# The first load of a streaming sum of reciprocals, made in two transfers

## The chip, the cores and the metric

The kernel runs on one core of a Trainium2 chip. Its time is the device time of one execution in microseconds; where several runs are compared, the median counts. The core has a tensor engine (PE), a vector engine (DVE), a scalar engine (ACT), a general engine (POOL) and an engine that here only issues transfers (SP). Sixteen DMA engines move data between the chip's main memory and the core's own memory.

## The reference

The input has 32 x 512 rows of 1024 positive float32 numbers, 67.1 MB. The output is one number per row:

```python
def reference(x: np.ndarray) -> np.ndarray:
    return np.sum(1.0 / x, axis=-1).astype(np.float32)
```

## The kernel before, in words

The 16384 rows are dealt to 128 partitions, 128 rows to each, so "row r" below means 128 rows of the input, one per partition. A partition's rows lie one after the other in main memory, so that a load of n rows is one run of n x 4096 bytes in each partition.

**The arithmetic.** A row is cut into halves a and b of 512 columns, and 1/a + 1/b is worked out as (a + b) / (ab), so that one reciprocal serves two elements. The product ab is made by POOL (token P, line 197), or for a few rows by DVE (tokens V and W, line 218). ACT makes the reciprocal of the product as exp(-ln(ab)): token L (line 240) is the logarithm and E (line 249) the exponential. DVE then multiplies, sums along the row and writes one number (token R, line 265, followed by a short read of the accumulator). Rows go one of two ways at the end. In the first, E writes the reciprocal to a bank of the matmul memory (E with @bank), and R multiplies it with both halves of the row. In the second, PE adds the halves a + b in a bank by two matmuls with an identity matrix (token S, line 230), E writes in place, and R multiplies the two. Where DVE makes the product, PE mostly copies the second half into a bank first (token C, line 207), so that DVE reads one operand from there.

**The order.** All of it is written out in one string, PLAN (lines 37 to 72). Each token is one step; its letter names the operation, the number the row, +2 two rows at once and @n the bank. Each engine carries out its own tokens strictly in the order in which they stand. An engine that waits at a token therefore holds up all its later ones. Which instruction waits for which is worked out by `note` (lines 133 to 162), row by row: a reader of a row waits for the one transfer that brings it.

**The loads.** Token Dn (lines 179 to 191) loads the next n rows into a ring of 40 rows. SP issues them on one queue, in order. The first three tokens load 12, 15 and 13 rows and fill the ring without a wait; each later load waits on SP until the rows that it overwrites have been used. The transfers take eight completion semaphores in turn, so that a transfer also waits for the one issued eight before it. Loads grow smaller towards the end, down to half rows: the last two rows are treated as four units of half the width.

**Around the change.** The first tokens after the loads are P0+2, C3@3, S2@0, V3, P2, L0, L1, C11@3, S3@1, E0@6, E1@7, P4+2, V11, L2, L3, R0, S6@2, E2, E3, R1. So POOL's first three steps are P0+2, P2 and P4+2; PE's are C3, S2, C11, S3 and S6; DVE's are V3, V11, R0 and R1. Rows 0 to 3 are used by P0+2, C3, V3, P2, S2 and S3, and later by R0 to R3; row 11 is used by C11 and V11.

Of the kernel before, what the change touches and what calls it, by code (L numbers as in the profile page):

```python
# [11 lines left out]
def kernel(  # L12
# [22 lines left out]


    PLAN = """
        D12 D15 D13 P0+2 C3@3 S2@0 V3 P2 L0@0 L1@1 C11@3 S3@1 E0@6 E1@7 P4+2 V11 L2@3 L3@2
        R0 S6@2 E2 E3 R1 P6+2 L4+2@4 R2 R3 E4+2@6 S7@0 P8+2 L6+2@8 R4 S10@1 E6+2 R5 D7 P10
        L8+2@10 R6 R7 S11@2 E8+2@6 L10+2@6 R8 E10+2 R9 R10 R11 P12+2 C19@3 S14@0 V19 P14+2  # L40
        L12+2@12 S15@1 E12+2@6 S18@2 R12 P16+2 L14+2@16 R13 E14+2 R14 P18 L16+2@18 R15 S19@0
# [271 lines left out]
```

## Time and profile before

| | us |
|---|---|
| time, median of 9 runs | 169.22 (168.93 to 169.68) |
| the profiled execution's own time | 169.26 |
| its span | 167.2 |
| PE, ACT, POOL, DVE busy in the span | 132.6, 132.9, 128.1, 128.0 |
| load of the first 12 rows, from issue to landing | 17.4 |
| load of the next 15 rows, from issue to landing | 35.1 |
| load of the next 13 rows, from issue to landing | 50.4 |

The span is the time from the first to the last thing that the profile records on the core; the execution's own time is 2.06 us longer. "Busy" counts the time in which an engine carries out instructions; an engine that waits at a semaphore is idle. A chain of waits names, from the last instruction back, what released each step; where a transfer is named, the time from its issue to its landing is shown, whether it moved or stood in the queue. A landing is the moment at which the transfer's semaphore is complete, that is, when the last of the 16 DMA engines has finished its share. Each DMA engine carries the same eight partitions of a transfer, one packet for each partition.

### The profile page before, as it was taken

The numbers are of one execution on the slowest core, as the hardware profiler recorded it, in microseconds if no ns is written. First come the engines' busy times: TensorE is split into PE (matmuls) and PEld (weight loads), VectorE is DVE, ScalarE is ACT, GpSimd is POOL, SyncE is SP. The second block draws the span as 40 slices with busy tenths as digits, with TensorE's granted clock in tenths as the row PEclk, the third lists the DMA queues.
The fourth block names the chain that finished last, engine by engine and source line by source line (L and its number), as shares of the span: only waits on it lengthen the run. The fifth ranks groups of instructions, "written<-read, shape, count | busy, mean of one in ns | idle before, by whom it ended". The sixth has DMA issues, their size and how long they took to land.

```text
span 167.2 us, 1332 instructions
## 1 busy us (share of the span) xinstructions
PE 132.6 (79%) x292; PEld 54.8 (33%) x292; DVE 128.0 (77%) x283; ACT 132.9 (79%) x161; POOL 128.1 (77%) x80
## 2 busy tenths in 40 slices
PE   0000699939989999977998999999799669989692
PEld 0000243314433434322433434344244133424261
DVE  0000129863789989887798898799999989999994
ACT  3000096926999999986999997999899999999992
POOL 1000699129999999949999997966899997979970
PEclk9999999996999999999999999999999999999999
DMA  6998999999998999999999999999999999999910
GB/s 200 470 459 376 470 470 470 411 403 446 433 408 365 432 445 415 470 396 439 423 447 431 431 404 437 431 437 423 411 439 420 408 425 412 427 406 411 396 73 16
DMA packets 4616, 67.26 MB, mean 402 GB/s; under 512 B 512, under 2 KB 640, under 8 KB 2176
## 3 DMA queue, kind: packets, MB, share of 16 engines
q1 hardware_dynamic: 4608, 67.18, 94.8%
q14 instruction: 6, 0.05, 0.1%
q8 instruction: 2, 0.03, 0.1%
HBM read 67.11 MB, written 0.07 MB: 402 GB/s over the span
## 4 chain that ended last, share of the span: by engine, by line
DMA 50%; DVE 17%; POOL 11%; issue 8%; PE 8%; ACT 4%; DVEq 0%; SPq 0%; ACTq 0%; POOLq 0%
DMA ring<-in_x_dram 50%; POOL prod L197 11%; DVE ring L265 10%; PE ps L230 5%; DVE prod L265 4%; PE ps L207 3%; DVE prod L218 2%; ACT prod L240 2%; ACT ps L249 1%; DVE sums L265 1%; ACT prod L249 1%; DVEq L308 0%; SPq L185 0%; ACTq L240 0%; POOLq L197 0%
## 5 line engine op out<-in xcount | busy, mean ns | idle before, releaser
L197 POOL TENSOR_TENSOR prod<-ring 128x1024 f32<-128x1024 f32 (+2 forms) x74 | 127.4, 1753 | 33.8 <-DMA ring<-in_x_dram 31.8
L230 PE MATMUL ps<-ring,ident 128*128 128x512 f32 (+1 forms) x260 | 117.7, 600 | 5.4 <-DVE sums L265 4.2
L240 ACT ACTIVATE prod<-prod 128x1024 f32<-128x1024 f32 (+2 forms) x80 | 69.1, 876 | 27.4 <-POOL prod L197 26.5
L265 DVE CUSTOM_DVE_ANT_1 ring<-ring,ps 128x1024 f32<-128x1024 f32 (+1 forms) x65 | 76.4, 1209 | 8.8 <-ACT ps L249 8.8
L230 PEld LDWEIGHTS ps<-ring,ident 128*128 128x128 f32 x260 | 49.1, 194 | 72.8 <-issue 50.9
L265 DVE CUSTOM_DVE_ANT_0 prod<-prod,ps 128x512 f32<-128x512 f32 (+1 forms) x63 | 40.6, 678 | 1.2 <-ACT prod L249 1.2
L207 PE MATMUL ps<-ring,ident 128*128 128x512 f32 x32 | 18.4, 666 | 26.1 <-DMA ring<-in_x_dram 26.1
L249 ACT ACTIVATE ps<-prod 128x1024 f32<-128x1024 f32 (+2 forms) x40 | 33.9, 854 | 2.4 <-DVE sums L265 1.6
L249 ACT ACTIVATE prod<-prod 128x1024 f32<-128x1024 f32 (+2 forms) x40 | 34.6, 875 | 0.8
L218 DVE TENSOR_TENSOR prod<-ring,ps 128x512 f32<-128x512 f32 x16 | 10.9, 686 | 26.8 <-PE ps L207 26.6
L207 PEld LDWEIGHTS ps<-ring,ident 128*128 128x128 f32 x32 | 5.7, 201 | 36.1 <-issue 21.5
L265 DVE DVE_READ_ACCUMULATOR2_ANT sums<- 128x1 f32 x130 | 10.8, 83 | 0.0
L218 DVE TENSOR_TENSOR prod<-ring 128x512 f32<-128x512 f32 (+1 forms) x7 | 4.3, 635 | 0.0
L83 ACT ACT_TABLE_LOAD x1 | 1.3, 1283 | 0.7 <-PEq L297 0.7
L265 DVE CUSTOM_DVE_ANT_0 prod<-prod,ps,sums 128x256 f32<-128x256 f32 x2 | 0.9, 478 | 0.0
masks.py:197 POOL MEMSET ident<- 128x128 f32 x1 | 0.2, 205 | 0.3 <-POOLq L297 0.3
masks.py:199 POOL TENSOR_SCALAR_AFFINE_SELECT ident<-ident 128x128 f32<-128x128 f32 x1 | 0.3, 294 | 0.1
L297 POOL MEMSET const-float32-0.0<- 128x1 f32 x1 | 0.1, 100 | 0.2 <-issue 0.2
L297 POOL MEMSET const-bfloat16-1.0<- 128x1 bf16 x1 | 0.1, 103 | 0.0
L297 POOL MEMSET const-uint8-127<- 128x1 uint8 x1 | 0.1, 103 | 0.0
L297 POOL MEMSET const-float32-1.0<- 128x1 f32 x1 | 0.1, 100 | 0.0
## 6 DMA issues: line engine op xcount, KB each, us to landing
ring<-in_x_dram SPq DMA_DIRECT2D x2, 4096.0 KB, 32.3
ring<-in_x_dram SPq DMA_DIRECT2D x1, 7680.0 KB, 35.1
ring<-in_x_dram SPq DMA_DIRECT2D x2, 3584.0 KB, 30.1
ring<-in_x_dram SPq DMA_DIRECT2D x1, 6656.0 KB, 50.4
ring<-in_x_dram SPq DMA_DIRECT2D x1, 6144.0 KB, 17.4
ring<-in_x_dram SPq DMA_DIRECT2D x3, 2048.0 KB, 34.6
ring<-in_x_dram SPq DMA_DIRECT2D x2, 3072.0 KB, 32.3
ring<-in_x_dram SPq DMA_DIRECT2D x1, 5120.0 KB, 27.2
```

What stands on the lines that cost most here:

```text
L83: nc.scalar.add_instruction(mybir.InstLoadActFuncSet(name=nc.get_next_instruction_name(), act_func_set_id=act_sets.index("natural_log_exp_ ...
L197: inst = nc.gpsimd.tensor_tensor(out=prod[:, p : p + m, :w], in0=ring[:, a : a + m, at : at + w], in1=ring[:, a : a + m, at + w : at + 2 * w],
L207: inst = nc.tensor.matmul(ps[:, b, : place(r)[2]], lhsT=ident, rhs=xs(r, 1), start=True, stop=True,)
L218: inst = nc.vector.tensor_tensor(out=prod[:, p, :w], in0=xs(r, 0), in1=in1, op=mult)
L230: inst = nc.tensor.matmul(ps[:, b, : place(r)[2]], lhsT=ident, rhs=xs(r, h), start=h == 0, stop=h == 1,)
L240: inst = nc.scalar.activation(out=pg, in_=pg, func=Ln, scale=S)
L249: inst = nc.scalar.activation(out=rc, in_=pg, func=Exp, scale=-1.0)
L265: inst = nc.vector.tensor_tensor_reduce(out=row, in0=row, in1=other, scale=S, scalar=total if q in summed else 0.0, op0=mult, op1=add, acc ...
L297: nc = _bacc.Bacc("TRN2", target_bir_lowering=False, num_devices=1)
```

## The change

The first load of 12 rows is issued as two loads, of 4 and of 8 rows. Every other token and its place stay the same, and the order on PE, DVE, ACT and POOL is unchanged. SP issues 32 loads instead of 31. What waits for what follows: the users of rows 0 to 3 wait for the first transfer, those of rows 4 to 11 for the second. Each later transfer takes the next semaphore in turn, and its wait is for the transfer eight before it in the new count.

```diff
     PLAN = """
-        D12 D15 D13 P0+2 C3@3 S2@0 V3 P2 L0@0 L1@1 C11@3 S3@1 E0@6 E1@7 P4+2 V11 L2@3 L3@2
+        D4 D8 D15 D13 P0+2 C3@3 S2@0 V3 P2 L0@0 L1@1 C11@3 S3@1 E0@6 E1@7 P4+2 V11 L2@3 L3@2
         R0 S6@2 E2 E3 R1 P6+2 L4+2@4 R2 R3 E4+2@6 S7@0 P8+2 L6+2@8 R4 S10@1 E6+2 R5 D7 P10
```

## The prediction

> **What bounds the kernel now.** I read, in this order: the slices and DMA queue of the page, to see whether any resource is full all the time; the timeline of POOL, PE, ACT and DVE around the first landings, to see what an earlier landing could move; the chain that ended last; and the queue of SP, to see whether a load is ever issued too late.
>
> The page's span, its DMA slices and its queue row come first.
>
> ```profile
> span 167.2 us, 1332 instructions
> ...
> DMA  6998999999998999999999999999999999999910
> ...
> q1 hardware_dynamic: 4608, 67.18, 94.8%
> ```
>
> The load queue is busy 94.8% of 167.2 us, 158.5 us, and its only slack is before the first packet and in the last slices. All 16 DMA engines stream from about 1.75 us to the last landing at 161.49 us. No compute engine passes 79%.
>
> Next the timeline at the first two landings, one engine after the other: POOL, PE, ACT, DVE.
>
> ```profile
> 18.25 11.79 POOL L197 TENSOR_TENSOR prod<-ring 128x1024 f32<-128x1024 f32 x6 [16.94 <-DMA ring<-in_x_dram]
> 36.38 24.69 POOL L197 TENSOR_TENSOR prod<-ring 128x1024 f32<-128x1024 f32 x12 [6.35 <-DMA ring<-in_x_dram]
> ...
> 28.05 5.52 PE L230 MATMUL ps<-ring,ident 128*128 128x512 f32 x12 [0.24 <-DVE sums L265]
> 36.36 1.68 PE L207 MATMUL ps<-ring,ident 128*128 128x512 f32 x2 [2.79 <-DMA ring<-in_x_dram]
> ...
> 33.59 1.06 ACT L249 ACTIVATE prod<-prod 128x1024 f32<-128x1024 f32 x1
> ...
> 36.12 0.08 DVE L265 DVE_READ_ACCUMULATOR2_ANT sums<- 128x1 f32 x1
> ```
>
> Columns: start, duration, engine, line, count, and idle time before with its releaser. The 12 rows land at 18.2 us. POOL has multiplied them by 30.03, PE has finished at 33.57, ACT at 34.65, and DVE reads its last accumulator at 36.12 to 36.20. The 15-row load lands at 36.31. So at 36.3 every engine has finished every row it has, and waits for data.
>
> Then the last long DMA piece of the chain, and SP's issues between 28 and 60 us.
>
> ```profile
> 100.06 34.96 DMA ring<-in_x_dram
> 135.02 0.14 issue
> 135.16 1.10 PE ps L207 x2
> ...
> 31.02 21.39 SPq L185 DMA_DIRECT2D ring<-in_x_dram  x3
> ```
>
> The end hangs on the landing at 135.02 us: PE copies and sums from it, DVE takes over and runs almost without a gap to 164.8. The issue at 100.06 is not what made that landing late, since 35 us of transfers stood ahead of it in the queue. The three issues of rows 40 to 63 come at 31.02, 46.81 and 52.08, while the first 40 rows land until 52.06 and the next 7 and 10 rows until 60.8 and 74.0: so the queue still holds 21, 14 and 22 us of transfers at those moments. The last load of all is issued at 153.80 and lands at 161.49. An earlier issue cannot make the stream earlier.
>
> **The change, part by part.** The profiled execution took 169.26 us, span 167.2 and 2.06 around it; the median of the nine runs is 169.22, so sums against 169.26 stand 0.04 high.
>
> 1. *One more issue on SP.* The first three take 0.38 to 0.42 us each, at 0.74, 1.18 and 1.65. The issues of the 15 and 13 rows move back by about 0.45 us, to 1.65 and 2.1. They are needed at 18 and 36 us, so the cover is 16 us and the cost is 0. The first issue stays at 0.74.
>
> 2. *More packets in the stream.* From the trace's record of each DMA packet: the 12 rows of one partition are one packet of 49,152 bytes, 128 such packets in all, eight on each DMA engine. After the change each DMA engine has eight of 16,384 and eight of 32,768 instead. Shortest packets of those sizes elsewhere in the trace: 0.611, 1.213 and 1.815 us. So 0.611 + 1.213 - 1.815 = 0.009 us per partition, with the usual 0.613 for the small one 0.011, times eight = 0.09 us per engine. One more completion packet adds 0.009 us. Between transfers nothing else is paid: the 15 rows land 18.14 us after the 12, and 8 x 2.267 us are 18.14. Cost 0.1 us on the full stream, with nothing beside it: the landing at 36.31 and all later ones move to +0.1.
>
> 3. *The start of the stream.* The first packet of each engine took 2.18 to 2.90 us, 0.6 us more than 1.815 in the mean; the second and later ones 1.815 to 1.92. I price it as paid once, as before: 0. Bounds: it shrinks with the packet to a third (-0.4), or is paid again by the first packets of the second transfer (+0.6). I take 0 because the first packets of the 15-row load, which also follow a transfer on a running queue, take 2.267 like all their others.
>
> 4. *Rows 0 to 3 land early.* First packets begin at 1.75 to 2.78; 0.6 + 8 x 0.613 = 5.5 us later, plus 0.3 us from last packet to semaphore (17.83 to 18.17 before), gives about 8.6 us. What can then run: POOL's product of rows 0 and 1 (2.35 us) and row 2 (1.28), PE's copy of row 3 and sum of row 2 (18.31 to 23.5, 5.2 us), DVE's V3, ACT's logs and exponentials of rows 0 to 3.
>
> 5. *Two waits move to the second transfer.* POOL's P4 waits for the 8 rows: behind it all POOL products, and ACT's L4. PE's C11 waits for them: behind it S3, though its row is there, and then S6 and S7. DVE's V11 waits for C11, and R0 to R3 stand behind V11. So no reduction of a row runs before 18.3 either. All that is won by then is 3.6 us of POOL, 5.2 us of PE and 4.5 us of ACT. POOL ends its first 12 rows at about 18.3 + 8.3 = 26.6 instead of 30.0, DVE its last of them some 3 to 5 us before 36.2.
>
> 6. *What is late next.* At 36.4 all engines wait for the 15 rows, exactly as before; POOL's wait grows from 6.35 to about 9.8 us and nothing else changes. The ring slots come free earlier, so the 7-row load is issued at about 27 instead of 31.02, behind 25 us of queue instead of 21. Value 0.
>
> 7. *PE's clock.* The granted clock is 0.50 from 36.80 to 40.20 us, after PE's pause of 2.79. A longer pause can put the drop ahead of 36.4, so that the first copy takes 2.04 us (as at 18.31) instead of 1.68. V19 on DVE then starts 0.4 late, but DVE's next operation waits 2.15 us for ACT, which covers it. Cost 0; without that cover 0.4.
>
> Sum: 0 + 0.1 + 0 + 0 + 0 = +0.1 us, 169.26 + 0.1 = 169.36, less the 0.04 to the median: **169.3 us**.
>
> The Trainium skill (Perfetto Trace Analysis, DMA Optimizations) says that splitting transfers may let the task end sooner if the DMA engines are generally idle; here the row reads 94.8% busy, so the rule's condition fails, and with it the gain. The same skill (DMA: Bandwidth & Descriptors, Anatomy of one DMA) gives about 2.0 us of fixed cost for each DMA; if the stream paid that, the sum would be 171.3 us, but landings 18.14 us apart for 18.14 us of packets show that a queued transfer pays none of it here.
>
> **The rivals.**
>
> - *The second transfer pays a start of its own* (slower). Place: the first packets of the 8 rows, at about 7 us. Price 0.6, with step 2 +0.7: 169.9 us. It decides over the forecast from 0.25 us of excess on the slowest engine. For: no trace shows a small packet at the very start of the stream, where the packets took 0.6 us too long. Against: the 15- and 13-row loads start without it.
> - *The head start survives* (faster). If the engines did not run dry at 36.3, POOL's 3.6 us would travel on to the end: 169.3 - 3.6 = 165.7. Against: 6.35 us of idle POOL and 2.79 us of idle PE before 36.4, waiting for DMA, and again 2.49 us of POOL at 74.1.
> - *A luckier order of the DMA engines* (slightly faster). Engines end the first transfer between 16.93 and 17.83 us, and a landing waits for the last. If smaller first packets even this out by half, -0.45: 168.9. For: step 3's excess differs by 0.7 us between engines. Against: the start order, which the issue sets, remains.
> - *The clock of PE* (slower): step 7 without its cover, +0.1 + 0.4: 169.7.
> - *The change does nothing at all*: 169.2, not to be told from the forecast.
>
> **How the numbers follow.** Forecast with the idle case 64%; second start 14%; clock 6%; luckier engines 11%; head start 5%. A measurement of this kernel tells about 0.2% (0.34 us) from no change. Forecast: 61 same, 3 slower. Second start: 12 slower, 2 same. Clock: 5 slower, 1 same. Engines: 8 faster, 3 same. Head start: 5 faster. Together faster 0.13, same 0.67, slower 0.20. The likeliest case alone is 169.0 to 169.6. The range takes in the luckier engines and the second start and leaves out the head start: 168.8 to 169.9.
>
> **What would show it.** Right: a first landing at 8 to 9 us, a second at 18.2 to 18.4, the 15 rows at 36.3 to 36.6; POOL idle some 10 us before that; the last landing 0.1 us later. Wrong: a first packet of the second transfer above 1.3 us; the 15 rows landing before 36.0 or after 36.8; an engine still at work on the first 12 rows when they land; or an end that moves apart from the landing at 135.02.

## The result

| | before | after |
|---|---|---|
| time, median | 169.41 us (31 runs, 168.93 to 170.16) | 168.86 us (10 runs, 168.78 to 169.02) |
| ratio, 95% interval | | 0.9968 (0.9958 to 0.9978) |
| the profiled execution: time, span | 169.26, 167.2 | 168.86, 167.1 |
| last load landed | 161.49 us | 161.25 us |
| output issued | 164.86 us | 164.64 us |

The change makes the kernel 0.55 us faster, 0.32%. The first nine of the 31 runs are those of the table before the change (169.22), on which the forecast was built; against them the gain is 0.36 us. The forecast was 169.3 us and no measurable change. The time lies inside the stated range and next to one of the rivals (168.9), but the sign of the most likely case was missed.

The page of the kernel after, its span, DMA slices, packets and load queue:

```profile
span 167.1 us, 1335 instructions
...
DMA  5999999999999998999999999999999999999910
...
DMA packets 4760, 67.26 MB, mean 403 GB/s; under 512 B 528, under 2 KB 656, under 8 KB 2192
...
q1 hardware_dynamic: 4752, 67.18, 94.7%
```

The queue carries 144 packets more than before (4752 against 4608): those that step 2 counted, 128 of data and 16 of completion. It is as full as it was (94.7% against 94.8%).

The timeline of POOL, PE and DVE after, up to the first product of the 15-row load (start, duration, and in brackets the idle time before, with what ended it):

```profile
8.18 3.57 POOL L197 TENSOR_TENSOR prod<-ring 128x1024 f32<-128x1024 f32 x2 [6.88 <-DMA ring<-in_x_dram]
17.86 8.23 POOL L197 TENSOR_TENSOR prod<-ring 128x1024 f32<-128x1024 f32 x4 [6.10 <-DMA ring<-in_x_dram]
36.00 2.34 POOL L197 TENSOR_TENSOR prod<-ring 128x1024 f32<-128x1024 f32 x1 [9.91 <-DMA ring<-in_x_dram]
...
35.98 2.08 PE L207 MATMUL ps<-ring,ident 128*128 128x512 f32 x2 [6.64 <-DMA ring<-in_x_dram]
...
31.71 0.08 DVE L265 DVE_READ_ACCUMULATOR2_ANT sums<- 128x1 f32 x1
```

The head start is there, and it is absorbed: POOL's wait for the 15 rows grew from 6.35 to 9.91 us, DVE stops at 31.79 instead of 36.20. But the two landings themselves are earlier. POOL starts on the 15 rows at 36.00 instead of 36.38, and on rows 4 to 11 at 17.86, while it had rows 0 to 11 at 18.25 before.

The DMA view of the first 3 us after, with the loads issued in them (size, time from issue to landing):

```profile
ring<-in_x_dram SPq DMA_DIRECT2D x1, 7680.0 KB, 34.3
ring<-in_x_dram SPq DMA_DIRECT2D x1, 6656.0 KB, 49.6
ring<-in_x_dram SPq DMA_DIRECT2D x1, 4096.0 KB, 16.6
ring<-in_x_dram SPq DMA_DIRECT2D x1, 2048.0 KB, 7.4
```

With issues at 0.74, 1.16, 1.63 and 2.10 us these are landings at 8.11, 17.79, 35.94 and 51.69. Before, 12, 15 and 13 rows landed at 18.17, 36.31 and 52.06. The stream runs 0.37 us ahead although it carries 0.1 us more packets, and it does so from the first 12 rows on.

The chain that ended last, and the issue of the output, after:

```profile
99.73 35.08 DMA ring<-in_x_dram
134.81 0.14 issue
134.95 1.10 PE ps L207 x2
...
164.64 0.34 SPq L282 DMA_DIRECT2D out_dram<-sums  x1
```

The landing that stood at 135.02 us is now at 134.81, 0.21 us earlier, and the issue of the output moves with it, from 164.86 to 164.64. So the end still hangs on the stream, as the prediction read it.

### The profile page after: what moved, and what is told of

Its sections match the earlier page's. It is cut to its first block, busy times and chain, and to the rows that moved or that the text cites. A ratio compares the mean times of both kernels' runs of the same rounds, so it can differ in the third digit from the quotient of the medians.

```text
span 167.1 us, 1335 instructions
## 1 busy us (share of the span) xinstructions
PE 134.1 (80%) x292; PEld 55.9 (33%) x292; DVE 128.3 (77%) x283; ACT 133.0 (80%) x161; POOL 128.1 (77%) x80
## 3 DMA queue, kind: packets, MB, share of 16 engines
q1 hardware_dynamic: 4752, 67.18, 94.7%
## 4 chain that ended last, share of the span: by engine, by line
DMA 60%; DVE 16%; PE 15%; issue 3%; ACT 2%; SPq 1%; DVEq 0%; ACTq 0%
DMA ring<-in_x_dram 60%; PE ps L230 11%; DVE ring L265 10%; DVE prod L265 4%; PE ps L207 4%; DVE prod L218 2%; ACT prod L240 1%; DVE sums L265 1%; ACT prod L249 1%; ACT ps L249 1%; SPq L185 1%; DVEq L308 0%; ACTq L240 0%
## 5 line engine op out<-in xcount | busy, mean ns | idle before, releaser
L230 PEld LDWEIGHTS ps<-ring,ident 128*128 128x128 f32 x260 | 50.0, 196 | 72.4 <-issue 52.9
L207 PE MATMUL ps<-ring,ident 128*128 128x512 f32 x32 | 19.8, 709 | 25.4 <-DMA ring<-in_x_dram 25.4
L207 PEld LDWEIGHTS ps<-ring,ident 128*128 128x128 f32 x32 | 5.9, 212 | 35.2 <-issue 16.8
```

Source lines behind the costliest of these rows:

```text
L207: inst = nc.tensor.matmul(ps[:, b, : place(r)[2]], lhsT=ident, rhs=xs(r, 1), start=True, stop=True,)
L230: inst = nc.tensor.matmul(ps[:, b, : place(r)[2]], lhsT=ident, rhs=xs(r, h), start=h == 0, stop=h == 1,)
```

## The experiments

Two theories stood at the outset. **A, the start:** the slowest of the 16 DMA engines gets through its first packets sooner when they are short, and the end follows the stream. **B, the head start:** work done on early rows reaches the end in some way that the waits do not show. After the first four runs a third was needed. **C, outside the span:** part of the gain is time that the profile's span does not contain. "Outside the span" below is an execution's time less its own span, as a mean over a kernel's runs; it was 1.86 us in the ten runs of the changed kernel. "Too long" is the time of a packet over the usual time of its size in the same trace. The packet records do not name the DMA engine; the first 16 packets by start are taken as the first of each of the 16 engines. The spread is the time between the first and the last of the 16 engines that report a landing.

**The kernel before, once more.**

> The kernel before, unchanged, for a second profile of it and for the width of the comparison. Theory A (the slowest DMA engine starts the stream more slowly when the first packets are long; the end follows): ratio 1.000 within 0.001; first packets of 49,152 bytes again 0.5 to 0.8 us too long in the mean; the 12 rows land between 18.1 and 18.5 us. Theory B (the early rows let the engines run ahead) says the same of this run. If the 12 rows land at 17.8 here, A has lost its evidence, since the profile before would then have been a late one by chance.

Median 169.27 us, ratio 0.9996 (0.9987 to 1.0006). The 12 rows landed at 18.14 us, first packets were 0.63 us too long in the mean (0.64 in the first profile), and the 16 DMA engines reached that landing with a spread of 0.94 us (0.87). The late landing of before is no accident of one profile.

**The first 12 rows as 1 and 11.**

```diff
-        D12 D15 D13 P0+2 ...
+        D1 D11 D15 D13 P0+2 ...
```

> The first 12 rows in transfers of 1 and 11 rows. No step of any engine can use row 0 alone (POOL's first product is of rows 0 and 1, PE's first copy of row 3), so there is no head start at all, but the first packets are short, 4,096 bytes. Theory A: first packets at most 0.4 us too long in the mean, the 12 rows land at 17.6 to 17.9 us, time 0.3 to 0.6 us below the kernel before, ratio 0.9965 to 0.998. Theory B: no head start, no gain: ratio 1.000 to 1.001 (the additional packets cost 0.1 us).

168.97 us, ratio 0.998 (0.9971 to 0.9989). First packets of 4,096 bytes were 0.28 us too long in the mean, and the 12 rows landed at 17.65 us. The first packets of the 11-row transfer behind them, from 3.31 us on, were 0.13 us too long in the mean and up to 0.42, so here the start was not paid by the very first packets alone. The mean span fell by 0.17 us. There is a gain in the span with no early row that any step can use. That is A; B expected none.

**The first 12 rows as 8 and 4.**

```diff
-        D12 D15 D13 P0+2 ...
+        D8 D4 D15 D13 P0+2 ...
```

> The first 12 rows in transfers of 8 and 4 rows. First packets of 32,768 bytes, between those of the two kernels; eight rows land at about 12.5 us, so that three of POOL's products and all that hangs on rows 0 to 7 except what stands behind C11 on PE can run early. Theory A: first packets 0.45 to 0.6 us too long in the mean, the 12 rows land at 17.9 to 18.2 us, ratio 0.998 to 1.000. Theory B: POOL's head start is larger than with 4 rows (5 us against 3.6), so the gain is at least that of the change: ratio 0.997 or less.

169.17 us, ratio 0.9992 (0.9982 to 1.0001). First packets of 32,768 bytes were 0.57 us too long, the spread was 0.90 us, and the 12 rows landed at 18.25 us, slightly later than A expected. POOL's timeline in this run:

```profile
13.43 11.78 POOL L197 TENSOR_TENSOR prod<-ring 128x1024 f32<-128x1024 f32 x6 [12.13 <-DMA ring<-in_x_dram]
36.47 4.66 POOL L197 TENSOR_TENSOR prod<-ring 128x1024 f32<-128x1024 f32 x2 [11.26 <-DMA ring<-in_x_dram]
```

POOL is 4.8 us ahead of the kernel before, and its wait grows to 11.26 us. The mean span, 167.29 us, equals that of the kernel before in the same comparison (167.30). The larger head start is worth nothing: B falls.

**A small load ahead of the 12 rows.**

```diff
     with tc.manual_schedule():
+        nc.sync.dma_start(out=sums, in_=x_v[:, F - 1, :F])
         for op, r, n, b in ops:
```

> An additional load of 128 columns (512 bytes per partition, into the sums, which are overwritten later) is issued ahead of the load of 12 rows; all else as before. It costs 8 x 0.027 us of stream, and the 12 rows are issued about 0.45 us later. No head start. Theory A in the form that only the very first packets of the stream pay: the 49,152-byte packets take 1.82 to 1.95 us from the first on, and the 12 rows land at 17.9 to 18.2 us: ratio 0.998 to 1.000. Theory A in the form that long packets are slow at the start whatever stands before them: they take 2.4 us again, the 12 rows land at 18.6 to 18.8, ratio 1.002 to 1.004. Theory B: no head start, later landing, ratio 1.001 to 1.003.

169.67 us, ratio 1.0022 (1.0013 to 1.0031). The first 512-byte packets paid next to nothing (0.029 us against 0.025), and the 49,152-byte packets behind them, starting at 2.25 to 3.21 us, took 2.57 us in the mean, 0.76 too long. The 12 rows landed at 18.65 us. So it is not the very first packet as such that pays: in this run a set of long packets near the start paid its excess even behind half a microsecond of short ones. Packets of 32,768 bytes that begin at 7.3 us in the changed kernel took 1.213, the shortest for their size in any part of the trace.

In these four runs the kernels with 32 loads had 1.83 to 1.89 us outside the span, those with 31 had 2.05. This gave theory C, and four more runs.

**The changed kernel again.**

> The changed kernel once more, beside the three others. Theory A (start): the spread of the 16 DMA engines at the landing of the 12 rows is again about half of that before (0.43 against 0.87 and 0.94 us), the 12 rows land at 17.7 to 17.9 us, the mean span is 0.2 to 0.3 us shorter than that of the kernel before. Theory C (a share of the gain lies outside the span and goes with the number of transfers): 1.84 to 1.90 us outside the span, against 2.05 for the kernel before. Both together: ratio 0.9965 to 0.9975.

168.88 us, ratio 0.9974 (0.9965 to 0.9984). The 12 rows landed at 17.83 us with a spread of 0.69 us, less narrow than 0.43 but below that of before. Mean span 166.98 against 167.21, outside 1.93 against 2.13: the two shares are 0.23 and 0.20 us.

**The same two transfers, with no head start.**

```diff
-                    q, at, w = place(r)
+                    g = {0: 8, 4: 0}.get(r, r)
+                    q, at, w = place(g)
...
-                    note("SP", inst, writes=rows(r, m))
+                    note("SP", inst, writes=rows(g, m))
```

> As the changed kernel, transfers of 4 and 8 rows, but the first brings rows 8 to 11 and the second rows 0 to 7. Every engine's first step needs one of rows 0 to 3, so nothing can run before the second landing: the same packets in the same order, without a head start. Theory A: 12 rows land at 17.7 to 17.9 us, span 0.2 to 0.3 us shorter than before. Theory C: outside the span 1.84 to 1.90. A and C: ratio 0.9965 to 0.998. Theory B (head start): the gain inside the span is gone, the span is that of the kernel before or 0.1 longer; with C ratio 0.999.

168.87 us, ratio 0.997 (0.9959 to 0.9982). POOL's timeline in this run:

```profile
17.84 11.78 POOL L198 TENSOR_TENSOR prod<-ring 128x1024 f32<-128x1024 f32 x6 [16.54 <-DMA ring<-in_x_dram]
35.99 2.34 POOL L198 TENSOR_TENSOR prod<-ring 128x1024 f32<-128x1024 f32 x1 [6.37 <-DMA ring<-in_x_dram]
```

POOL now does all six products in one stretch from 17.84 us, as before the change from 18.25, and waits 6.37 us for the next load (6.35 before). There is no head start, and the time is that of the changed kernel to 0.01 us; the mean span is 167.02 us, against 166.98 in the changed kernel and 167.21 before. The early rows add nothing to the gain that can be measured: it comes with the start of the stream.

**One load in the middle split instead.**

```diff
-  ... R29 D8 P34 ...
+  ... R29 D4 D4 P34 ...
```

> The start as before, with one load of 12 rows; instead the first load of 8 rows in the middle (rows 64 to 71) is made in two of 4 rows. 32 loads as in the changed kernel. Theory A: start and landing of the 12 rows as before (18.1 to 18.3), span as before, 0.0 to 0.1 longer. Theory C: outside the span 1.84 to 1.90, so 0.15 to 0.2 us less than before, ratio 0.9988 to 0.9995. If C is wrong, 2.05 outside and ratio 1.000 to 1.001.

169.19 us, ratio 0.9992 (0.9984 to 1.0001). The same rows of POOL's timeline:

```profile
18.27 11.79 POOL L197 TENSOR_TENSOR prod<-ring 128x1024 f32<-128x1024 f32 x6 [16.97 <-DMA ring<-in_x_dram]
36.40 2.34 POOL L197 TENSOR_TENSOR prod<-ring 128x1024 f32<-128x1024 f32 x1 [6.34 <-DMA ring<-in_x_dram]
```

The start is that of before. The span is 167.36 us (167.21 before), the time outside it 1.84 (2.13): the additional transfer costs about 0.15 in the span and saves 0.3 outside. This kernel and the last two have the same number of transfers and ran on one chip; they differ by where the split is. 169.10 to 169.30 us stands against 168.76 to 169.02 and 168.74 to 168.94: a short start is worth 0.3 us.

**The changed kernel with two late loads merged.**

```diff
-  S80@3 D1 D1 L82@7 ...
+  S80@3 D2 L82@7 ...
```

> As the changed kernel, with two neighbouring loads of one row late in the kernel (rows 120 and 121) merged into one, so that the number of loads is 31 as before. Theory A: the 12 rows land at 17.7 to 17.9, span 0.2 to 0.3 shorter than before (up to 0.3 may be lost again because row 120 lands with row 121). Theory C: outside the span 2.05 again, so ratio 0.998 to 0.999. If C is wrong, 1.85 outside and ratio 0.9965 to 0.9975.

170.65 us, ratio 1.0093 (1.0073 to 1.0114). The start kept its gain (12 rows at 17.83 us) and the time outside the span went back to 2.17, as C expected with 31 loads. But the merge itself cost 1.8 us of mean span (168.73 against 166.98 in the changed kernel), not 0.3. Its six runs fall into two groups, with spans of 168.3 to 168.5 and 169.4 to 169.5 us; the profile is of the first. POOL's timeline between 150 and 156 us in this run:

```profile
149.92 2.56 POOL L197 TENSOR_TENSOR prod<-ring 128x512 f32<-128x512 f32 x2
153.62 2.51 POOL L197 TENSOR_TENSOR prod<-ring 128x512 f32<-128x512 f32 x2 [1.14 <-DMA ring<-in_x_dram]
```

The same stretch of the changed kernel, where five products follow one another without a wait:

```profile
149.87 6.36 POOL L197 TENSOR_TENSOR prod<-ring 128x512 f32<-128x512 f32 x5
```

Row 120 now lands with row 121, at 153.55 instead of 152.27 us, and POOL, which has no slack there, stops for 1.14 us. A delay of 1.3 us in one row this late is not absorbed, while 3.6 us of head start at 8 us is. What the second group lost on top no profile shows.

**33 loads, and 30.** The first splits two loads of 8 rows in the middle, the second is the kernel before with the same late merge.

```diff
-  ... R29 D8 P34 ... R37 D8 P42 ...
+  ... R29 D4 D4 P34 ... R37 D4 D4 P42 ...
```

> The start as before with one load of 12 rows; two loads of 8 rows in the middle are each made in two of 4 rows, so that there are 33 loads. The time outside the span was 2.05 to 2.13 us with 31 loads and 1.83 to 1.93 with 32. If each additional load takes 0.2 us off it, it is 1.65 here and the ratio 0.998 to 0.999; if it is a step between 31 and 32, it is 1.83 to 1.93 and the ratio 0.999 to 1.000. Span as before or up to 0.2 longer (two more sets of packets at 0.1 us).

> The kernel before with the loads of rows 120 and 121 merged, 30 loads in all. The span grows by 1 to 1.8 us, as it did with the same merge in the changed kernel, and is not what is asked. Outside the span: 2.05 to 2.2 us if there is a step between 31 and 32 loads, 2.25 to 2.35 if each load counts, 1.83 to 1.93 if only 31 is slow.

33 loads: 169.29 us, ratio 0.9993 (0.9983 to 1.0002), span 167.52 against 167.26, outside 1.77. 30 loads: 171.5 us, ratio 1.0118 (1.0098 to 1.0138), outside 1.81; the mean span grew by 2.3 us, to 169.57, more than the 1 to 1.8 expected. Neither a step between 31 and 32 nor a price per load fits; of the three readings put down for the 30 loads, "only 31 is slow" came nearest:

| loads (with the output one transfer more) | outside the span, us |
|---|---|
| 30 | 1.81 |
| 31 (three comparisons of the kernel before; the changed kernel with a merge) | 2.05, 2.13, 2.13; 2.17 |
| 32 (six kernels) | 1.83 to 1.93 |
| 33 (two middle splits; the next run) | 1.77, 1.78 |

The means for 31 loads hide two groups. In the 75 executions of the kernel before in these three comparisons, the time outside the span was 1.74 to 1.82 us in nine and 1.97 to 2.29 us in the other 66 (spans are on record to 0.1 us). So the longer time with 31 loads is usual, not certain. With the output, 31 loads are 32 transfers, four for each of the eight semaphores; whether that matters no run tests.

**The first 12 rows as 1, 3 and 8.**

```diff
-        D12 D15 D13 P0+2 ...
+        D1 D3 D8 D15 D13 P0+2 ...
```

> The first 12 rows in transfers of 1, 3 and 8 rows, 33 loads. First packets of 4,096 bytes as in the run with 1 and 11 rows, the head start of the changed kernel. Theory A: first packets 0.2 to 0.4 us too long, 12 rows at 17.6 to 17.9 us, span 0.1 to 0.3 shorter than that of the kernel before, outside the span 1.83 to 1.93 (or 1.65, if each load counts): ratio 0.9965 to 0.998, no better than the changed kernel. A ratio under 0.996 would mean that start and head start add up.

168.87 us, ratio 0.997 (0.9959 to 0.9981); first packets 0.42 us too long, 12 rows at 17.77 us, span 167.08 against 167.26. Still shorter first packets do not add to the gain.

## Why the prediction was wrong

**Right:** step 1 (SP's additional issue cost nothing), step 2 (144 packets; two splits in the middle cost 0.26 us of mean span, 0.13 each, against 0.1 in the sum), the first landing (8.11 against 8.6), step 5 (no reduction before the second landing: DVE's first R starts at 20.61), and step 6, the heart of the argument: the head start ends in longer waits. The run with rows 8 to 11 first shows this directly. The second transfer paid no start of its own: its first packets took 1.213 us, as elsewhere. Step 7 holds as well: PE's granted clock averages 0.96 in the two comparisons of the changed kernel and 0.99 in that run, at the same time.

**Wrong, the first of two: step 3.** It priced the start of the stream at 0, "as paid once, as before", with -0.4 as the lower bound if the excess shrinks to a third with the packet. The landings moved by nearly that much, and the prediction's own sign of being wrong came: the 15 rows landed before 36.0, at 35.94. But the size of the bound was met by luck: the mean excess did shrink, though not to a third. From the trace's packet records:

| first packets, bytes | too long, mean us (one value per profile) | 12 rows landed, us |
|---|---|---|
| 49,152 (five profiles) | 0.63 to 0.72 | 18.06 to 18.20 |
| 32,768 | 0.57 | 18.25 |
| 16,384 (four profiles) | 0.36 to 0.54 | 17.77 to 17.83 |
| 4,096 (two profiles) | 0.28, 0.42 | 17.65, 17.77 |

The mean excess alone does not set the landing: 0.54 too long went with 17.77 us, and 0.57 with 18.25. What goes with the landing is the spread of the 16 engines: 0.75 to 0.94 us with first packets of 49,152 bytes and 0.90 with 32,768, but 0.43 to 0.69 with 16,384 and 0.55 and 0.58 with 4,096. The first engine was done at 17.20 to 17.36 us with the longest packets and at 17.14 to 17.36 with those of 16,384; it is the last one that moved.

A landing waits for the last engine. In the kernel before, the last one began its second packet at 5.14 us, 1.57 us later than a start at 1.75 and a packet of 1.815 would give; in the changed kernel at 3.50, 1.14 us later. The difference, 0.43, less the packets of step 2, 0.09, is 0.34 us; the landing moved by 0.37. I took 0 because the 15-row load starts without any excess. That load is of a stream already running and says nothing of how one begins. The rival with "a luckier order of the DMA engines" had the mechanism, halving the spread, and 168.9 us; what spoke against it, that the order of starts remains, does not matter: first packets began at 1.75 to 2.78 us before and at 1.75 to 2.68 after, and what changed is how long they took. What sets the order of starts no record here shows. That the rival's 168.9 was met is partly luck: it gave 0.45 us to the start, of which about half reached the end, and the rest of the gain lies outside the span.

Of these 0.37 us, 0.24 are left at the last landing and 0.22 at the issue of the output. The mean over the 16 engines had gained less from the first: 0.14 us at the 12 rows (17.69 to 17.55), and 0.22 at the last load (160.12 to 159.90). On the way some DMA engines fall behind: at the last landing of the kernel before, 13 of the 16 lie within 1.1 us of one another, and the other three end 0.8 to 1.0 us after the latest of them; in the kernel after it is the same picture, with three engines 0.6 to 0.8 us late. In both traces single packets are 0.34 to 0.66 us too long where the core's own instructions are loaded, at about 54, 66, 73, 113 and 118 us. That these packets belong to the late engines, and that such delays swallow a part of a better start, is argued, not tested.

**Wrong, the second: a term that the sum lacked.** The prediction added 2.06 us for what lies around the span as if the change could not touch it. In the mean it is 1.86 to 1.93 in the changed kernel and 2.05 to 2.13 in the kernel before. The kernel with a split in the middle isolates this: its start and span are no better than before, and it still has 0.3 us less outside. What happens in that time no profile here shows; only the dependence on the number of transfers is measured, and that 31 loads is the odd one stands on the counts from 30 to 33 alone.

Together, in round figures: +0.1 for the packets, -0.43 for the start, +0.1 given back on the way and -0.2 outside the span make -0.43 us; the two comparisons measured -0.46 and -0.55.

The rule that was weighed against this change (the Trainium skill, Perfetto Trace Analysis, DMA Optimizations: splitting transfers may let the task end sooner if the DMA engines are generally idle) was read too far. Its condition fails here, at 94.8% busy, and the work that started sooner was indeed worth nothing; but a rule that says when a split may help does not say that it cannot help otherwise. The gain came by a way that the rule does not name. The 2.0 us for each DMA that the prediction set beside its sum stand, on its page, in a section on transfers that the general engine issues, and the loads here are issued by SP; the landings 18.14 us apart decide without that figure.

## What to carry to other kernels

Where a stream of loads is the bound, look at how it starts: read the first packet of each DMA engine against a later one of the same size, ask how far the slowest engine falls behind there, and price a change in that packet's size by that, not by how the same queue behaves later. Data that arrived early did not help here, because a wait further on drained every engine; look for such a wait first. And compare the time outside the span between kernels too, because an execution is more than its profile.

## What was not expected of the hardware

- The first packets of an otherwise idle queue of 4,096 bytes and more took 0.28 to 0.72 us too long in the mean, the longest the most, and a leading transfer of 512-byte packets did not cure it (0.76 us on the long packets behind it). Why the size matters is open.
- With 31 loads and one store the execution took in the mean about 0.2 to 0.35 us more outside the span than with 30, 32 or 33 loads, though nine of 75 executions did not.
- The kernel before scatters more than the changed one: 168.93 to 170.16 us in 31 runs against 168.78 to 169.02 in 10. The two groups of the time outside its span, 0.15 us or more apart, may be a part of that.
